# Sums over a head's channels as two fp32r products of split squares, and a pair's values requested after its queries

## The chip, the cores and the metric

The kernel runs on one core of a Trainium2 chip. A core has five engines with their own instruction streams: TensorE (PE in the profile, with its weight loads as PEld), VectorE (DVE), ScalarE (ACT), GpSimd (POOL) and SyncE (SP, which here only issues DMAs). Each works its stream in the order in which it was recorded, and waits on semaphores for the others. The metric is the device time of one execution in microseconds (us). Each kernel's time is a median over several executions.

## The reference

One layer over 528 tokens (16 learned ones and 512 of the input) of 1024 channels, in fp32. A projection of the normed input feeds a recurrent branch (RWKV-7, 8 heads of 64 channels), an attention branch with forgetting (8 heads of 64) and two gates; the branches are mixed and added, and an MLP with squared ReLU follows.

```python
kk = hv(k * k_k)                                   # recurrent branch
kk = kk / jnp.maximum(jnp.sqrt(jnp.sum(kk * kk, axis=-1, keepdims=True)), 1e-12)
...
bonus = jnp.sum(hv(r) * hv(k) * r_k, axis=-1, keepdims=True) * hv(v)

def head_rmsnorm(t, g):                            # queries and keys of attention
    tf = t.astype(jnp.float32)
    return tf * lax.rsqrt(jnp.mean(tf * tf, axis=-1, keepdims=True) + NORM_EPS) * g
```

These are the sums over a head's 64 channels: the length of each recurrent key, the bonus, and the mean square of each query and key.

## The kernel before, in words

Features lie with 128 channels, that is two heads (a "pair"), on the partitions, and tokens along the free dimension. The kernel has three stages. A short first one norms the input and splits it into a high and a low fp32r part (`uhi`, `ulo`). The second, until about 401 us, holds the projections, the recurrence and attention. The third mixes the branches (tiles `po`, `pd`), adds the residual and computes the MLP.

In the second stage products with weights are made as three fp32r products (high by high, high by low, low by high; tile `pj`, line 579), while small products of the branches are single fp32 ones. A sum over a head's channels is a product with `ones_blk`, a 128 by 128 matrix of two blocks of ones, in fp32: line 680 (`pssq`, queries and keys of attention), line 906 (`pkk`, recurrent keys) and line 940 (`pbn`, the bonus, with the matrix scaled by `r_k` beforehand, line 934).

TensorE's order in this stage is recorded by a planner, `Turns`. Each piece of work is a Python generator, a stream: `recurrent` (rank 1), `attention` (2), `fox_features` (3, norms and transposes attention's inputs), `divided` (4, splits the branches' results), `chain` (0), `group_norm` (4) and `projections` (8). A stream yields a function that gives the time when its next input is ready by a cost table; the planner takes the stream of lowest rank that is ready by its own count of TensorE's time. `projections`, ready nearly always, so fills TensorE wherever the others wait. It takes its jobs from a list ordered by rank and request; a job may carry an event (`need`) that must have come before it starts, and then all later jobs stand behind it. The 16 gate blocks (rank 9) are the last of the list. The planner settles TensorE's order; a tile scheduler orders the other engines.

The recurrence treats two groups of two pairs. For each pair it makes `decay`, `keys`, `rows`, `scores` and `bonus`, for a group `inverse`; then the group's `chain` runs over nine chunks, and each chunk is a ring of dependent steps: `pch<-uv,L` (line 1102), a copy on VectorE, `pch<-Rs,Tt` (1108), two copies, `pch<-uv,bkT` (1130), an addition. The chunk's output goes to `py` (1136, 1087). After chunks 4 and 8 `group_norm` works on four chunks: a reduction, a square, a second reduction, eleven tiny steps of an inverse root and a scaling (lines 1146 to 1156), the transposes `pyt` (1161) and products `pg` (1164), then two copies and two operations for each pair (1169 to 1172), whose result is split for the third stage (276). The keys of the fourth pair are requested once the third pair's are normed, and held until that pair's `rows`, which wait for the first chain.

The first products of the third stage are `po` (line 1260); the first of them needs the four recurrent results `ys` that are split last.

Two tiles with one tag share memory in turn. The tags concerned by the change are "KT" (the scaled keys, then a work area of `inverse`), "lc" and "tha" (cumulated decay and gate of the recurrence).

Of the kernel before, what the change touches and what calls it, by code (L numbers as in the profile page):

```python
# [19 lines left out]
T = 528  # L20
NM = 16
S = 512
# [167 lines left out]
def kernel(ctx, tc, ht, x, win, par, cst, gain, lora, wout, wo, wup, wdn, out, dbg=None):  # L190
# [16 lines left out]
    pr = cp.tile([128, N_PAR], F32, name="pr")  # L207
    ident, ones_blk, tmask, cmask = (cs[:, 128 * i:128 * i + 128] for i in range(4))
    mask16 = cs[:, 512:]

# [64 lines left out]
    def split(hi, lo, x):  # L275
        return A.copy(hi, x), V.tensor_tensor(lo, x, hi.bitcast(F32), ALU.subtract)  # L276

    def passes(w, x):
# [9 lines left out]
    with ExitStack() as st:  # L288
# [337 lines left out]
        def forget(prev):  # L626
# [10 lines left out]
            forgot.done = True  # L637

        class Fox:

# [32 lines left out]
            def normed(self, d, parts, gcol):  # L673
                yield d["in"]
                f, sq = d["f"], d["sq"]
                yield lambda: max(ck.ready(sq), banks(len(parts)))
                pin = None
                for a0, a1 in parts:
                    pq = psm("pssq")[:, :a1 - a0]
                    mm(pq, ones_blk, sq[:, a0:a1], start=True, stop=True)  # L680
                    pin = pin or pinned(d["s"])
                    after(act(sq[:, a0:a1], pq, AF.Ln, bias=eps, scale=1.0 / 64), pin)
                c0 = parts[0][0]
# [168 lines left out]
        class Pair:  # L852
# [20 lines left out]
            def decay(self):  # L873
                p = self.p
                lw = load_lora(p, 0, 1)

# [20 lines left out]
            def keys(self):  # L897

                p = self.p
                okr, thr, kp, pinv = self.okk[:, PADT:], self.tha[:, PADT:], self.sg, v9(self.lc)  # L900
                self.sq = sq = rp.tile([128, TP], F32, name="sq")
                s_ = act(sq[:, :T], okr, AF.Square, scale=self.col(C_KK))
                yield lambda: max(ck.ready(sq), banks(2))
                for hc in (slice(0, HT), slice(HT, T)):
                    pq = psm("pkk")[:, :HT]
                    mm(pq, ones_blk, sq[:, hc], start=True, stop=True)
                    V.tensor_scalar(sq[:, hc], pq, 1e-24, None, ALU.max)
# [13 lines left out]
                V.tensor_tensor(KT, BK, self.P[:, :, 63:64].unsqueeze(2).to_broadcast([128, NCH, 2, 64]), ALU.mult)  # L921

            def rows(self):
# [8 lines left out]
                G.tensor_tensor(self.sq[:, :S], self.orr[:, 64:], self.sg[:, 64:], ALU.mult)  # L932
                self.rkb = rp.tile([128, 128], F32, name="rkb")
                after(V.tensor_scalar(self.rkb, ones_blk, self.col(C_RK), None, ALU.mult), last["DVE"])

            def bonus(self):
                rkb = self.rkb
                yield lambda: max(ck.ready(rkb, self.sq), banks(1))
                bp = psm("pbn")
                mm(bp, rkb, self.sq[:, :S], start=True, stop=True)  # L940
                self.bv = bv = rp.tile([128, S], F32, name="bv", bufs=2)
# [3 lines left out]
            def scores(self):  # L945
# [5 lines left out]
                for c0 in range(0, NCH, 3):  # L951
# [14 lines left out]
                    for hs, os in zip(hss, hss[::-1]):  # L966
                        A.copy(bkT[hs, c0:c0 + 3, 64:], pb[os, :3, 64:])

        def inverse(g, Bms, late):


            n2 = 2 * NCH
            Ain = rp.tile([128, 32, 32], F32, name="Ain", tag="Ain")
# [76 lines left out]
            for q in (0, 2):  # L1050
                A.copy(T2[qs[q], :, 32:64], p1[qs[q]])

        def chain(g, prs):
# [555 lines left out]
```

## Time and profile before

| | |
|---|---|
| median of 3 runs | 826.56 us (826.28 to 828.94) |
| the profiled execution | 826.42 us, its span 824.6 us |
| TensorE busy | 808.5 us, 98% |
| VectorE, ScalarE, GpSimd busy | 606.5, 452.7, 120.6 us |
| granted clock of TensorE, mean | 0.998 |
| head sums on TensorE: `pssq`, `pkk`, `pbn` | 8.4, 4.2, 4.1 us |

The page's fifth part groups instructions by source line, engine and tile. [...] An fp32 product shows as two records. The chain of waits follows the work that ended last back through time. In the timeline each row gives start and duration in us, engine, line, operation, output and inputs, shape, count, and in brackets the idle time before it and what ended that.

### The profile page before, as it was taken

How to read it: one execution, taken by the hardware profiler on the slowest of the kernel's cores; microseconds unless marked ns; L12 is line 12 of the kernel's file. 1: busy time of each engine (PE TensorE's matmuls, PEld its weight loads, DVE VectorE, ACT ScalarE, POOL GpSimd, SP SyncE). 2: the span in 40 equal slices, each digit the busy share in tenths (PEclk: the TensorE clock that was granted, in tenths of full speed). 3: DMA queues.
4: the chain of work that ended last, by engine and by line, in shares of the span. 5: the costliest groups of instructions: out<-in, count | busy, mean ns of one | idle time of the engine just before them, and what ended most of it. 6: DMA issues, size and time to landing. Idle time of an engine off the chain costs nothing.

```text
span 824.6 us, 15506 instructions
## 1 busy us (share of the span) xinstructions
PE 808.5 (98%) x5886; PEld 667.4 (81%) x5886; DVE 606.5 (74%) x1196; ACT 452.7 (55%) x941; POOL 120.6 (15%) x124
## 2 busy tenths in 40 slices
PE   8989999998999999999999999999999999999998
PEld 6979887876987787678888889888888888888886
DVE  6787985687879855875366655875698679867988
ACT  7757538756575457754456534664445434543452
POOL 1021100010011000000032003100740074017300
PEclk9999999999999999999999999999999999999999
DMA  7222221211211412223687405523642365337532
GB/s 232 82 71 71 77 92 48 87 40 65 79 52 52 129 41 66 77 78 116 224 287 227 156 0 154 176 80 113 219 149 82 115 208 159 81 115 228 146 99 76
DMA packets 51483, 95.88 MB, mean 116 GB/s; under 512 B 5832, under 2 KB 7240, under 8 KB 51408
## 3 DMA queue, kind: packets, MB, share of 16 engines
q1 hardware_dynamic: 47680, 86.37, 33.2%
q0 software_dynamic: 1280, 4.20, 1.7%
q10 hardware_dynamic: 2448, 4.33, 1.5%
q8 instruction: 46, 0.75, 0.4%
q14 instruction: 29, 0.24, 0.1%
HBM read 88.56 MB, written 6.31 MB: 115 GB/s over the span
## 4 chain that ended last, share of the span: by engine, by line
PE 86%; DVE 5%; ACT 5%; issue 2%; DMA 1%; SPq 0%; POOL 0%; DVEq 0%; ACTq 0%
PE pj L579 22%; PE po L1350 21%; PE po L1477 12%; PE po L1260 5%; PE pd L1477 5%; PE po L1322 3%; PE pj L394 1%; PE po L1291 1%; PE pd L1291 1%; PE psc L748 1%; PE py L802 1%; PE psr L957 1%; PE ppt L785 1%; PE pch L1108 1%; DVE wlo L549 1%
## 5 line engine op out<-in xcount | busy, mean ns | idle before, releaser
L579 PE MATMUL pj<-uhi,whi 128*128 128x264 f32 (+1 forms) x480 | 164.2, 342 | 0.0
L579 PE MATMUL pj<-uhi,wlo 128*128 128x264 f32 (+1 forms) x480 | 153.8, 320 | 2.5 <-DVE wlo L549 2.5
L579 PE MATMUL pj<-ulo,whi 128*128 128x264 f32 (+1 forms) x480 | 153.8, 320 | 0.0
L242 DVE TENSOR_TENSOR wlo<-wraw,whi 128x512 fp32r<-128x512 f32 x84 | 80.3, 966 | 35.5 <-ACT whi L242 35.5
L579 PEld LDWEIGHTS pj<-uhi,whi 128*128 128x128 f32 x480 | 90.7, 189 | 12.8 <-issue 4.4
L579 PEld LDWEIGHTS pj<-uhi,wlo 128*128 128x128 f32 x480 | 90.7, 189 | 9.5 <-DVE wlo L549 2.9
L579 PEld LDWEIGHTS pj<-ulo,whi 128*128 128x128 f32 x480 | 90.9, 189 | 6.7 <-issue 1.6
L1350 PE MATMUL po<-zlo,whi 128*128 128x512 f32 (+1 forms) x248 | 94.8, 382 | 0.0
L1350 PE MATMUL po<-zhi,wlo 128*128 128x512 f32 (+1 forms) x248 | 94.8, 382 | 0.0
L1350 PE MATMUL po<-zhi,whi 128*128 128x512 f32 (+1 forms) x248 | 94.8, 382 | 0.0
L242 ACT CAST whi<-wraw 128x512 fp32r<-128x512 f32 x84 | 51.4, 617 | 55.7 <-PE po L1350 25.6
L548 ACT CAST whi<-wraw 128x512 fp32r<-128x512 f32 x78 | 47.8, 617 | 42.3 <-PE pj L579 41.6
L549 DVE TENSOR_TENSOR wlo<-wraw,whi 128x512 fp32r<-128x512 f32 x78 | 52.7, 685 | 23.7 <-ACT whi L548 23.0
L276 ACT CAST whi<-t 128x512 fp32r<-128x512 f32 x64 | 39.9, 623 | 44.5 <-DVE wlo L276 27.3
L1477 PE MATMUL po<-wlo,fhi 128*128 128x512 f32 (+1 forms) x164 | 63.4, 387 | 0.1
L1399 POOL TENSOR_TENSOR t<-traw 128x512 f32<-128x512 f32 x24 | 38.2, 1608 | 171.6 <-DMA traw<-in_wdn 171.6
L1477 PE MATMUL po<-whi,flo 128*128 128x512 f32 (+1 forms) x164 | 62.9, 384 | 0.0
L1477 PE MATMUL po<-whi,fhi 128*128 128x512 f32 (+1 forms) x164 | 62.3, 384 | 0.0
L276 DVE TENSOR_TENSOR wlo<-t,whi 128x512 fp32r<-128x512 f32 x64 | 43.6, 690 | 24.2 <-ACT whi L276 24.0
L1366 ACT CAST fhi<-R 128x768 fp32r<-128x768 f32 (+1 forms) x32 | 30.2, 944 | 45.2 <-DVE R L1373 25.3
L1350 PEld LDWEIGHTS po<-zhi,wlo 128*128 128x128 f32 x248 | 46.6, 188 | 9.1
L1350 PEld LDWEIGHTS po<-zhi,whi 128*128 128x128 f32 x248 | 46.6, 188 | 9.0
(330 smaller groups left out, 1708.6 us busy)
## 6 DMA issues: line engine op xcount, KB each, us to landing
wraw<-in_win SPq DMA_DIRECT2D x84, 256.0 KB, 2.7
wraw<-in_wup SPq DMA_DIRECT2D x60, 256.0 KB, 3.1
wraw<-in_wdn SPq DMA_DIRECT2D x48, 256.0 KB, 2.7
traw<-in_wdn SPq DMA_DIRECT2D x48, 256.0 KB, 3.5
gd<-gt ACTq DMA_DIRECT2D x16, 256.0 KB, 2.2
wraw<-in_wout SPq DMA_DIRECT2D x16, 256.0 KB, 3.5
gl<-gd SPq DMA_DIRECT2D x16, 256.0 KB, 3.0
traw<-in_wdn POOLq DMA_DIRECT2D x16, 256.0 KB, 3.2
```

The lines of the kernel that those rows point to most:

```text
L242: casts.append((A.copy(hi, raw), low.tensor_tensor(lo, raw, hi.bitcast(F32), ALU.subtract)))
L276: return A.copy(hi, x), V.tensor_tensor(lo, x, hi.bitcast(F32), ALU.subtract)
L548: after(A.copy(hi, raw), last["ACT"])
L549: after(V.tensor_tensor(lo, raw, hi.bitcast(F32), ALU.subtract), last["DVE"])
L579: mm(po, a, b[:, k, a0:a1], start=n == 0, stop=n == 23)
L1260: mm(po, a, ys[k][:, b, :], start=n == 0, stop=n == 11)
L1291: mm(pd[i], a[:, k, 128 * i:128 * i + 128], b, start=k == 0 and n == 0, stop=k == 7 and n == 2)
L1322: mm(po, a[:, k, 128 * i:128 * i + 128], b[:, k, :], start=n == 0, stop=n == 23)
L1350: mm(po[:, t0:t1], a, b[:, k, t0:t1], start=n == 0, stop=n == 23)
L1366: A.copy(fhi[:, j, a:b], R[:, a:b])
L1399: eng.tensor_tensor(t, sums[c, pair] if c in (T1, T2) else c, d, ALU.add)
L1477: mm(x[i][:, cols], a[:, k, left, 128 * rows:128 * rows + 128], c[:, cols], start=start and k == 0 and n == 0, stop=stop and k == n_pairs ...
```

## The change

An fp32r copy `ones_r` of the matrix of ones is made once. Each of the three kinds of sum now splits its squares (for the bonus, the products) into a high part, cast to fp32r on ScalarE, and a low part, the difference, on GpSimd (for the bonus on VectorE), and adds two fp32r products in one accumulation (`summed`). The bonus scales its squares by `r_k` in the split, and the scaled matrix `rkb` is gone. The split parts are kept in memory of other tiles: in "KT" or in "lc" and "tha". Two flags, `held`, see to it that only one stream has each at a time: `decay` takes the second area, `keys`, `bonus` and `inverse` the first, `scores` or `inverse` give it back, and attention's `normed` takes whichever is free, or waits. Apart from that, the values of the second to fourth pair of attention are requested after its queries are normed, and no longer before.

```diff
+    def summed(po, hi, lo):
+        mm(po, ones_r, hi, start=True, stop=False)
+        mm(po, ones_r, lo, start=False, stop=True)
...
+        V.tensor_copy(ones_r, ones_blk)
...
+        held = [0, 0]
+
+        def hold(i):
+            yield lambda: math.inf if held[i] else 0.0
+            held[i] = 1
...
             def normed(self, d, parts, gcol):
                 yield d["in"]
                 f, sq = d["f"], d["sq"]
-                yield lambda: max(ck.ready(sq), banks(len(parts)))
+                c0 = parts[0][0]
+                yield lambda: math.inf if all(held) else 0.0
+                at = held[0]
+                held[at] = 1
+                if at:
+                    hl = rp.tile([128, 2, T], F32R, name="fhl", tag="KT")
+                    hi, lo = hl[:, 0, :], hl[:, 1, :]
+                else:
+                    hi, lo = (rp.tile([128, T], F32R, name="f" + tag, tag=tag) for tag in ("lc", "tha"))
+                d["s"] = A.copy(hi[:, c0:], sq[:, c0:])
+                for a0, a1 in parts:
+                    G.tensor_tensor(lo[:, a0:a1], sq[:, a0:a1], hi[:, a0:a1].bitcast(F32), ALU.subtract)
+                yield lambda: max(ck.ready(lo), banks(len(parts)))
                 pin = None
                 for a0, a1 in parts:
                     pq = psm("pssq")[:, :a1 - a0]
-                    mm(pq, ones_blk, sq[:, a0:a1], start=True, stop=True)
+                    summed(pq, hi[:, a0:a1], lo[:, a0:a1])
...
+                q = yield from x.normed(x.dq, SEQ, qg8)
+                x.q_done.done = True
                 if p > 0:
                     x.ask_values()
-                q = yield from x.normed(x.dq, SEQ, qg8)
-                x.q_done.done = True
...
             def decay(self):
                 p = self.p
+                yield from hold(0)
...
             def keys(self):
 
                 p = self.p
+                yield from hold(1)
...
-                yield lambda: max(ck.ready(sq), banks(2))
-                for hc in (slice(0, HT), slice(HT, T)):
+                hl = rp.tile([128, 2, T], F32R, name="hl", tag="KT")
+                hi, lo = hl[:, 0, :], hl[:, 1, :]
+                s_ = A.copy(hi, sq[:, :T])
+                for hc in parts:
+                    G.tensor_tensor(lo[:, hc], sq[:, hc], hi[:, hc].bitcast(F32), ALU.subtract)
+                yield lambda: max(ck.ready(hl), banks(2))
+                for hc in parts:
                     pq = psm("pkk")[:, :HT]
-                    mm(pq, ones_blk, sq[:, hc], start=True, stop=True)
+                    summed(pq, hi[:, hc], lo[:, hc])
...
             def bonus(self):
-                rkb = self.rkb
-                yield lambda: max(ck.ready(rkb, self.sq), banks(1))
+                yield from hold(1)
+                hl = rp.tile([128, 2, T], F32R, name="hl", tag="KT")
+                hi, lo = hl[:, 0, :S], hl[:, 1, :S]
+                A.activation(hi, self.sq[:, :S], AF.Copy, scale=self.col(C_RK))
+                V.scalar_tensor_tensor(lo, self.sq[:, :S], self.col(C_RK), hi.bitcast(F32), ALU.mult, ALU.subtract)
+                yield lambda: max(ck.ready(hl), banks(1))
                 bp = psm("pbn")
-                mm(bp, rkb, self.sq[:, :S], start=True, stop=True)
+                summed(bp, hi, lo)
+                held[1] = 0
...
         def inverse(g, Bms, late):
 
 
+            yield from hold(1)
```

The flags and the new waits enter the planner's choices, so that TensorE's whole order in the second stage is another one. Two places of it follow. The program's lines are shifted by 6 to 40 in the changed kernel (585 is 579 before, 1300 is 1260).

TensorE at the end of the second stage, before: the last output products of the chain and of attention (`py`), projections (`pj`), the transposes and products of the last group norm (`pyt`, `pg`), projections again, and the first products of the third stage (`po`).

```order
L1087 MATMUL py<-y_fx,Bm 64x64 x4
L799 MATMUL py<-pTm,vm 64x512 x2
...
L802 MATMUL py<-pT_4542,vt 64x128
L579 MATMUL pj<-uhi,whi 128x512
...
L1161 MATMUL pyt<-cs,ysq 128x128 x4
L1164 MATMUL pg<-lhi,lw_4209 128x256
...
L579 MATMUL pj<-uhi,whi 128x512
...
L1260 MATMUL po<-ys,whi 128x512 x2
```

The same end in the changed kernel, from the last projection on:

```order
L585 MATMUL pj<-uhi,wlo 128x512
L1170 MATMUL pch<-uv,bkT 64x64 x4
...
L1142 MATMUL pch<-uv,L_3154 64x64
...
L1148 MATMUL pch<-Rs,Tt 64x64 x4
...
L1142 MATMUL pch<-y_fx,L_3154 64x64
...
L826 MATMUL py<-pT_4918,vt 64x128
L1148 MATMUL pch<-Rs,Tt 64x64 x4
...
L1127 MATMUL py<-y_fx,Bm 64x64 x4
L1201 MATMUL pyt<-cs,ysq 128x128 x4
...
L1204 MATMUL pg<-lhi,lw_4561 128x256
L1300 MATMUL po<-ys,whi 128x512 x2
```

Before, 69 projection products stand ahead of the last group norm's transposes and 57 behind its products; now the last projection stands ahead of the seventh chunk's last step, and two chunks, attention's mixing and two group norms follow with none between.

TensorE at the end of the first chain, before: the eighth chunk's start to the first projection after the chain.

```order
L579 MATMUL pj<-uhi,wlo 128x512
L1102 MATMUL pch<-uv,L_662 64x64
...
L680 MATMUL pssq<-fsq,cs 128x512
L1130 MATMUL pch<-uv,bkT 64x64 x4
...
L748 MATMUL psc<-ka,qa 128x272 x2
L748 MATMUL psc<-ka,qa 128x256 x2
...
L1087 MATMUL py<-y_fx,Bm 64x64 x4
L579 MATMUL pj<-uhi,whi 128x264
```

And now:

```order
L772 MATMUL psc<-ka,qa 128x272 x2
L772 MATMUL psc<-ka,qa 128x256 x2
L1142 MATMUL pch<-uv,L_670 64x64
...
L585 MATMUL pj<-uhi,whi 128x512
...
L1148 MATMUL pch<-Rs,Tt 64x64 x4
L1127 MATMUL py<-uv,Bm 64x64 x4
L1105 MATMUL pvt<-cs,ov 64x128 x2
L585 MATMUL pj<-uhi,whi 128x264
...
L1170 MATMUL pch<-uv,bkT 64x64 x4
```

Before, the 37 rows between the two projections hold none; now projections stand between the chain's steps, up to its last output. Behind the first state product of the second chain lay 240 projection products of 512 columns and 30 of 264 before, and 78 and 48 now.

More of the change, by code (lines that the diff above doesn't have):

```diff
@@ L208 @@
     ident, ones_blk, tmask, cmask = (cs[:, 128 * i:128 * i + 128] for i in range(4))
+    ones_r = cp.tile([128, 128], F32R, name="ones_r")
     mask16 = cs[:, 512:]
@@ L679, in normed @@
                     pq = psm("pssq")[:, :a1 - a0]
-                    mm(pq, ones_blk, sq[:, a0:a1], start=True, stop=True)
+                    summed(pq, hi[:, a0:a1], lo[:, a0:a1])
                     pin = pin or pinned(d["s"])
                     after(act(sq[:, a0:a1], pq, AF.Ln, bias=eps, scale=1.0 / 64), pin)
-                c0 = parts[0][0]
+                held[at] = 0
                 d["s"] = act(sq[:, c0:], sq[:, c0:], AF.Exp, scale=-0.5)
@@ L921, in keys @@
                 V.tensor_tensor(KT, BK, self.P[:, :, 63:64].unsqueeze(2).to_broadcast([128, NCH, 2, 64]), ALU.mult)
+                held[0] = 0
             def rows(self):
@@ L967, in scores @@
                         A.copy(bkT[hs, c0:c0 + 3, 64:], pb[os, :3, 64:])
+                held[1] = 0
         def inverse(g, Bms, late):
+            yield from hold(1)
             n2 = 2 * NCH
@@ L1051, in inverse @@
                 A.copy(T2[qs[q], :, 32:64], p1[qs[q]])
+            held[1] = 0
         def chain(g, prs):
```

3 lines of the change are left out of this document (1 added, 2 removed).

## The prediction

> **What bounds the kernel now.** I read the page first, then the waits of TensorE, then the chain of waits between 350 and 401 us, where the recurrent stage ends.
>
> ```profile
> span 824.6 us, 15506 instructions
> PE 808.5 (98%) x5886; PEld 667.4 (81%) x5886; DVE 606.5 (74%) x1196; ACT 452.7 (55%) x941; POOL 120.6 (15%) x124
> ```
>
> TensorE (PE) is busy for 98% of the span, so its instruction stream, in its recorded order, is the clock of the whole kernel. Two things alone can move the time: PE work, and stretches in which PE's next instruction is not ready. The profiled execution took 826.4 us (span 824.6 and 1.8 around it), 0.1 under the median of the runs, 826.56; my sum starts at 826.4. What keeps PE fed through the recurrent stage are the projection products (pj, L579): they wait for nothing but their weights, and the planner lays them between the links of the slow chains. The chain of waits at the stage's end shows this stock (start, duration, engine, tile, line, count):
>
> ```profile
> 353.55 0.38 PE pch L1130 x8
> ...
> 354.17 1.59 PE pj L579 x6
> ...
> 357.96 2.77 PE pj L579 x12
> ...
> 362.83 1.59 PE pj L579 x6
> ...
> 365.03 0.89 PE pj L579 x3
> ...
> 367.45 0.38 PE py L1087 x8
> 367.83 1.00 PE py L799 x4
> 368.83 2.30 PE py L802 x16
> 371.14 15.89 PE pj L579 x69
> 387.02 0.44 PE pyt L1161 x4
> ...
> 388.18 12.92 PE pj L579 x57
> 401.10 9.07 PE po L1260 x40
> ```
>
> The last state product of the second chain ends at 367.83, attention's last at 371.14; then 69 projections run while VectorE and ScalarE work out the last group norm, and 57 more while its result is scaled and split. At 401.10 the output products (po) start, with all their operands long there. From 353.55 to 401.10 are 47.55 us; projections take 1.59 + 2.77 + 1.59 + 0.89 + 15.89 + 12.92 = 35.65 of them, the other PE rows 11.9.
>
> **The cheaper sums.** TensorE before and after a pair of fp32 sums of 264 columns (first fence), and two fp32 sums of 512 columns (second):
>
> ```profile
> 38.45 1.05 PE L906 MATMUL pkk<-sq,cs 128*128 128x264 f32 x4
> 39.14 0.48 PE L579 MATMUL pj<-uhi,whi 128*128 128x264 f32 x1
> 39.46 0.28 PE L579 MATMUL pj<-ulo,whi 128*128 128x264 f32 x1
> 39.58 0.28 PE L579 MATMUL pj<-uhi,wlo 128*128 128x264 f32 x1
> ```
>
> ```profile
> 65.39 1.02 PE L940 MATMUL pbn<-sq,rkb 128*128 128x512 f32 x2
> 66.25 1.02 PE L680 MATMUL pssq<-fsq,cs 128*128 128x512 f32 x2
> ```
>
> Rows overlap, so I count from start to start. An fp32r product of 264 columns costs 0.12 (39.46 to 39.58), one of 512 columns 15.89/69 = 0.23. The two fp32 sums cost 39.46 - 38.45 = 1.01 less the 0.12 of the projection product in it, 0.89; four fp32r products cost 0.48. There are eight such places (four keys of attention, four of the recurrence): 8 x 0.41 = 3.3 us. A 512-column sum costs 0.86 (65.39 to 66.25) against 2 x 0.23: 0.40 at eight places (four queries, four bonuses), 3.2. The projection after a sum started the next one 0.32 later instead of 0.12, a change of form worth 0.20; it is inside the 264-column price, and at the 512-column places I count 0.5 in all (0 to 1.6). Together **-7.0** (-6.5 to -8.1). All of it lies on PE, hence on the path while there is other PE work to take its place.
>
> **The splits.** Each of the 16 places now needs an extra cast on ScalarE and a subtraction on GpSimd (the bonus: VectorE, in place of scaling a matrix) before PE may sum.
>
> ```profile
> L932 POOL TENSOR_TENSOR sq<-orr,sg 128x512 f32<-128x512 f32 x4 | 7.5, 1876 | 24.4 <-DVE okk L913 15.5 <-DVE rsgy L222 8.6 <-DVE orr L310 0.3
> ```
>
> By this row, 1.88 for 512 columns and half for 264, that is 4 x 1.9 + 16 x 0.95 = 23 us of GpSimd, which the page has busy for 15% of the span; ScalarE, at 55%, has room for 16 casts. GpSimd runs in order: behind a split wait the next block's padding memsets and the BK product that the scores need. With cast and subtraction a place is late by at least the 1.9; uncovered everywhere, 16 x 1.9 = 30 us. The planner lays projections over it: thirty 264-column products (3.6 us) stand between the old and the new place of the first key sum. I charge **+0.9** for what slips through (0, all covered, to 4, a quarter us at each place). The buffers are lent too: while one stream holds "KT", or "lc" and "tha", the others stand. So the second chain comes later in PE's order: 240 projection products of 512 columns and 30 of 264 lay behind its first state product, now 78 and 48: 58.8 us of cover by the prices above has become 23.7.
>
> **The tail without cover.** That difference is spent earlier, and the end is bare: after the last projection come the rest of the seventh chain step, two whole steps, attention's last block, both group norms, and at once the output products. I work out the stretch that took 47.55 us, from the state product at 353.55:
>
> (a) To the end of the last state product (367.83): 14.3 us before, with 6.84 of projections in it. If those only filled time that the links need anyway, 14.3 stays; if they set the pace, 14.3 - 6.84 + 3.3 (attention's mixing, L799 and L802, which now lies inside) = 10.7. I take 12.7: each link's copies queue on VectorE behind attention's softmax, as before.
>
> (b) From there to the group norm's product:
>
> ```profile
> 368.70 0.68 DVE L1146 TENSOR_REDUCE st<-y_rw 128x8 f32<-128x512 f32 x1
> ...
> 374.04 0.69 DVE L549 TENSOR_TENSOR wlo<-wraw,whi 128x512 fp32r<-128x512 f32 x1
> ...
> 377.17 0.69 DVE L1156 TENSOR_TENSOR ysq<-y_rw,rsgy 128x512 f32<-128x512 f32 x1
> ...
> 392.54 0.69 DVE L276 TENSOR_TENSOR ys<-y_rw,ys 128x512 fp32r<-128x512 f32 x1 [0.24 <-ACT ys L276]
> ```
>
> 367.83 to 377.86 is 10.0. The row at 374.04 is the first of two weight splits that stand in between; without them 8.6, without two more splits of that size (other heads' results, as in the last row) 7.2. I take 8.7.
>
> (c) From the group norm's transposes (387.02) to the end of the last split (393.23) are 6.2, 5.5 without the weight split that stood between. Ten of the first twelve output products (10 x 0.23) can run before that split is there: 3.2 to 3.9, I take 3.7.
>
> Sum 25.1 us where PE has 11.9 of its own work: a stall of **+13.2** (9.2 to 16.3).
>
> **The clock.** TensorE's waits, and its clock (last but two) in windows around the longest wait at a chain's end:
>
> ```profile
> PE psc L748 <- DVE nm L759: 1.5, 1, 1.5
> ```
>
> ```profile
> 202.00:204.00 2.00, 1.15 (x4) 0.96 0.00 0
> 204.00:206.00 2.00, 2.00 (x20) 0.50 0.00 0
> 206.00:208.00 2.00, 2.00 (x14) 0.69 0.20 55
> ```
>
> A wait of 1.5 us was followed by a granted clock of 0.50 and 0.69: 2 x (0.04 + 0.50 + 0.31) = 1.7 us of work lost. Step (b) leaves PE idle for over 7 us, so the output products start slow (1.7), and the transposes and products of the group norm, on the path, lose 0.5: **+2.2** (0 if nothing dips; 4.6 with one more dip in the two chain steps, 1.7, and 0.7 on their links). [...]
>
> **The gap that closes.** The wait above came where the first chain ended with no projection among 37 rows of PE. The first block projected after it was a recurrent pair's keys:
>
> ```profile
> 209.88 0.49 DVE L310 SCALAR_TENSOR_TENSOR okk<-pj,pr,tm 128x264 f32<-128x264 f32 x1 [0.80 <-ACT tm L309]
> ```
>
> That job is held until the first chain is done, and stood first in line. Now the second group's keys are normed later against the chain, the held job comes to the front later, and projections lie in that place. So the wait and its dip go: **-3.2** (0 to -3.2). The values asked for later are three jobs that go past gate jobs, each with two weight loads on SyncE, two casts and two splits, covered by the same stock; if one came late, attention's transposes would (within the 4 above).
>
> Sum: 826.4 - 7.0 + 0.9 + 13.2 + 2.2 - 3.2 = **832.5 us**.
>
> **The rivals.** A difference under 0.3% (2.5 us) can't be told from none here. *Forecast: bare tail, slower*, chance 0.62, own range 829.2 to 836.5. *Faster*: with VectorE and ScalarE freed of weight splits, the last two steps and the norm close up, and the savings stand. It decides once the stall is under 7 us: with 6.0 and no dip, 826.4 - 7.0 - 3.2 + 6.0 + 0.9 = 823.1. For it: those engines have less to do in the tail. Against: my low end, 9.2, has foreign work taken out already. 0.10. *No change*: the stall is at that low end, 9.7 with the waits, and no dip: 826.4 - 10.2 + 9.7 + 0.4 = 826.3. For it: at 354 to 366 us projections followed every link, so links may be faster than they look. 0.18. *Slower still*: the lent buffers stall streams in mid-stage, the old gap gets a successor (0 gained), the tail is 14.5 with 3.2 of dips and 1.5 of waits: 826.4 - 7.0 + 14.5 + 3.2 + 1.5 = 838.6. For it: 16 new places wait for GpSimd, whose rows vary. 0.10.
>
> Faster 0.10, same 0.18, slower 0.62 + 0.10 = 0.72. The bounds alone give 824 to 845; the range leaves out the faster case and most of the last: 826.0 to 838.5.
>
> **What would show it.** Cheaper sums: PE busy down by about 7 us, pssq, pkk and pbn at 0.12 or 0.23 per product. Bare tail: no pj row in the last 25 us before the first po row, ten or more us of PE waits there on VectorE and ScalarE rows of the chain and the group norm, and a granted clock near 0.5 as po begins. Closed gap: no PE wait on nm near 200 us. I am wrong if PE's idle time between the last pj and the first dense po rows is under 8 us, or if PE shows new waits on hl, flc or ftha of several us.

## The result, and the profile after

The changed kernel takes 833.79 us (median of 4 runs, 833.13 to 835.41), the kernel before 827.34 (4 runs, 826.28 to 828.94): a ratio of 1.0071, with a 95% interval from 1.0049 to 1.0092. It is slower by 0.7%. The profiled execution took 833.66 us against 826.42, its span 831.9 against 824.6, so 7.3 us are to be found in it.

The head of the changed kernel's page:

```profile
span 831.9 us, 15539 instructions
PE 804.7 (97%) x5886; PEld 667.5 (80%) x5886; DVE 609.1 (73%) x1197; ACT 460.9 (55%) x957; POOL 136.2 (16%) x144
```

TensorE is busy for 3.8 us less, and its span is longer. The first output product of the dense row starts at 401.10 before and at 407.54 now; what follows takes 423.5 and 424.4 us. So the second stage holds nearly all of it. TensorE up to that product and behind it, before and then after (columns: window, its width, busy time, records, granted clock, DMA share, GB/s):

```profile
0.00:401.10 401.10, 388.93 (x3947) 1.00 0.27 83
401.10:824.60 423.50, 419.57 (x1941) 1.00 0.47 147
```

```profile
0.00:407.54 407.54, 384.33 (x3947) 0.98 0.26 84
407.54:831.90 424.36, 420.35 (x1940) 1.00 0.46 145
```

Width less busy time is idle time: 12.2 us before, 23.2 now. A second loss hides in busy time, the clock: in windows of 2 us, busy time times what the clock lacks of 1.00 sums to 1.7 before and 4.5 now. What is left I call work: 387.3 and 379.9. So the stage became 7.4 us lighter in work, and it lost 11.0 in waits and 2.8 in clock.

TensorE's waits now (line, what ended the wait; us in total, times, longest):

```profile
PE pyt L1201 <- DVE ysq L1196: 8.9, 1, 8.9
PE pw L1068 <- issue: 3.3, 2, 1.9
...
PE py L1176 <- ACT y_rw L1128: 1.2, 2, 0.8
PE psr L994 <- DVE tm L311: 1.1, 1, 1.1
```

The first row is the wait for the last group norm, which 15.89 us of projections covered before. The second is new in kind: TensorE stopped twice inside a burst of small products (lines 1065 and 1068, the inverse of each pair group), and the profile shows nothing that it waited for. The old first rows, wlo and nm, are gone from the list. No row names a split part (hl, fhl, flc, ftha).

The end of the stage in windows, from the last projection on (columns as above):

```profile
382.63:398.00 15.37, 11.35 (x145) 1.00 0.11 36
398.00:400.00 2.00, 0.00 (x0) 0.75 0.00 0
400.00:405.17 5.17, 0.00 (x1) 0.50 0.00 0
405.17:407.54 2.37, 2.37 (x11) 0.50 0.00 0
407.54:411.00 3.46, 3.46 (x12) 0.75 0.00 0
```

TensorE is idle for 4.0 + 2.0 + 5.2 = 11.2 us there, and the norm's products and the first output products then run at half clock.

### The profile page after: what moved, and what is told of

It reads as the page before. It is cut to its first block, busy times and chain, and to the rows that moved or that the text cites. A ratio compares the mean times of both kernels' runs of the same rounds, so it can differ in the third digit from the quotient of the medians.

```text
span 831.9 us, 15539 instructions
## 1 busy us (share of the span) xinstructions
PE 804.7 (97%) x5886; PEld 667.5 (80%) x5886; DVE 609.1 (73%) x1197; ACT 460.9 (55%) x957; POOL 136.2 (16%) x144
## 4 chain that ended last, share of the span: by engine, by line
PE 86%; DVE 7%; ACT 4%; issue 2%; DMA 1%; SPq 1%; DVEq 0%; ACTq 0%
PE pj L585 23%; PE po L1390 21%; PE po L1517 12%; PE po L1300 5%; PE pd L1517 5%; PE po L1362 3%; PE pj L399 1%; PE pd L1331 1%; PE po L1331 1%; PE py L826 1%; PE psc L772 1%; PE psr L994 1%; PE ppt L809 1%; PE pch L1148 1%; DVE wlo L555 1%
## 5 line engine op out<-in xcount | busy, mean ns | idle before, releaser
L585 PE MATMUL pj<-uhi,whi 128*128 128x264 f32 (+1 forms) x480 | 162.3, 338 | 0.8 <-DVE orr L315 0.8
L555 DVE TENSOR_TENSOR wlo<-wraw,whi 128x512 fp32r<-128x512 f32 x78 | 52.9, 690 | 23.2 <-ACT whi L554 22.8
L1390 PEld LDWEIGHTS po<-zlo,whi 128*128 128x128 f32 x248 | 46.6, 188 | 9.0
```

The source lines that it names most:

```text
L555: after(V.tensor_tensor(lo, raw, hi.bitcast(F32), ALU.subtract), last["DVE"])
L585: mm(po, a, b[:, k, a0:a1], start=n == 0, stop=n == 23)
L1390: mm(po[:, t0:t1], a, b[:, k, t0:t1], start=n == 0, stop=n == 23)
```

## The experiments

Each was timed against the kernel before on the same chip. The account of the stage, made as above, for all of them (us; the last column is the rest after idle time and clock, good to a few us only: e5 and e6 have 3946 records of the same products in the same order in it and come to 381.1 and 385.2). A trace is one execution, and the granted clock differs among the executions of one kernel: of 51 executions of the kernel before that were timed beside the experiments, the 13 with a mean clock of 0.998 took 826.7 us on average, the 24 with 0.996 took 828.6. The traced one has 0.998. So a difference of 2 us in the clock column can come from the execution that was traced, and not from the kernel.

| kernel | median | ratio to before | first output product | idle | clock | work |
|---|---|---|---|---|---|---|
| before | 827.34 | 1 | 401.1 | 12.2 | 1.7 | 387.3 |
| changed | 833.79 | 1.0071 | 407.5 | 23.2 | 4.5 | 379.9 |
| e1 values alone | 834.25 | 1.0072 | 408.6 | 14.5 | 6.4 | 387.6 |
| e2 sums alone | 834.27 | 1.0076 | 409.2 | 19.8 | 10.4 | 379.0 |
| e3 reserve | 839.70 | 1.0138 | 411.9 | 23.5 | 10.5 | 378.0 |
| e4 rounded, new plan | 828.84 | 1.0007 | 403.9 | 13.0 | 6.8 | 384.1 |
| e5 rounded, old order | 821.58 | 0.9917 | 395.8 | 11.3 | 3.4 | 381.1 |
| e6 split, old order | 846.22 | 1.0211 | 421.2 | 23.1 | 12.9 | 385.2 |
| e7 same, on VectorE | 843.48 | 1.0181 | 418.1 | 23.3 | 9.6 | 385.2 |
| e8 tail filled (7.7 of the work is filling) | 832.54 | 1.0057 | 407.6 | 15.3 | 4.0 | 388.2 |
| e9 fp32, new order | 834.04 | 1.0071 | 407.9 | 19.4 | 2.8 | 385.7 |
| e10 tail covered | 831.94 | 1.0045 | 408.4 | 19.9 | 8.4 | 380.1 |
| e11 one product, old order | 818.71 | 0.9884 | 393.8 | 13.8 | 3.3 | 376.7 |
| e12 shifted | 832.79 | 1.0050 | 403.2 | 19.9 | 2.8 | 380.6 |

### The two parts, each alone

e1 moves only the request of the values; e2 makes only the sums, with their splits and flags.

```diff
-                if p > 0:
-                    x.ask_values()
                 q = yield from x.normed(x.dq, SEQ, qg8)
                 x.q_done.done = True
+                if p > 0:
+                    x.ask_values()
```

> The kernel before with the second part of the change alone: values asked for after the queries are normed, sums as before. Theory A (the time follows TensorE's work and how much of the chain's end has projections behind it): its order still has 16.7 us of projections between the second chain's end and the last group norm's transposes and 9.7 us behind them, and the work is the same, so 825.5 to 829, no difference to tell. Rival B (the asking order itself starves attention and stalls TensorE): 830 or more.

> The changed kernel with values asked for before the queries are normed, as formerly; splits, lent buffers and the cheaper sums all stay. Theory A: work is 7.5 us less than before, and the order has 12.4 us of projections at the last group norm and none after it, so of the 25 us tail only some 3 us are bare: 821 to 825, faster than before. Rival B (splits and lending stall the streams, wherever the projections stand): near the changed kernel, 831 to 835.

Measured: 834.25 us, 1.0072 (1.0048 to 1.0096), and 834.27, 1.0076 (1.0054 to 1.0097). Theory A missed both times, and the times lie in the rivals' ranges: each part alone is as slow as the two together. The parts do not add up, so it can't be the tail's cover alone; and of e2's waits only one of 0.2 us names a split part. In e1 TensorE has the work of before, and waits and clock that before did not have. Its waits, and its clock around them:

```profile
PE pyt L1161 <- DVE ysq L1156: 2.9, 1, 2.9
PE pj L579 <- DVE wlo L549: 2.5, 1, 2.5
PE ppm L783 <- ACT pm L768: 2.3, 1, 2.3
```

```profile
52.00:56.00 4.00, 4.00 (x34) 0.57 0.74 231
182.00:185.00 3.00, 0.33 (x3) 1.00 0.00 0
185.00:189.00 4.00, 4.00 (x33) 0.57 0.01 4
```

Each of the three waits is followed by half clock. Windows laid on these stretches show 0.50 for 3.41 us behind the first two in time and for 6.83 behind the third, so they cost 1.7 to 3.4 us beside their own length. That is not fixed: the wait for wlo stands in the kernel before at the same place and with the same length (2.47 us there, 2.46 here), and the 2 us behind it ran at 1.00:

```profile
52.00:54.00 2.00, 2.00 (x19) 1.00 0.58 170
```

In e2 the tail has no wait at all; the largest one stands at 117 us, where the inverse's VectorE work comes late for TensorE:

```profile
PE pw L1059 <- DVE AX L1045: 6.9, 1, 6.9
PE pw L1068 <- issue: 2.1, 2, 1.2
```

What the three kernels share is only that the planner made a new order for the stage. That became the new theory A: the order, not the parts, costs the time.

### A reserve for the tail

In the changed kernel three gate blocks may start only when the second chain is done.

```diff
-            ask(9, B_GATE + i, gate_job(i), SEQ)
+            ask(9, B_GATE + i, gate_job(i), SEQ, need=chained[1] if i > 12 else None)
```

> The changed kernel with its last three gate blocks (16.6 us of projections) held back until the second chain has ended. Theory A (cover misplaced): the 11.6 us of stall and 3.7 us of slow clock at the last group norm go, but six chunks of the chain now have no projections between their steps, at about 1 us of stall each: 824 to 829. Rival (the stage has become bound by the length of the chain of splits and steps, not by where projections stand): what is gained at the end is lost in the chunks, 831 to 835.

Measured: 839.70 us, 1.0138 (1.0117 to 1.0159), slower than the changed kernel and than both answers. 72 projections now stand behind the chain (first fence, the chain of waits), and the chunks before it are bare (second fence, TensorE's waits):

```profile
394.19 16.55 PE pj L585 x72
```

```profile
PE ppt L807 <- ACT pm L792: 3.3, 1, 3.3
PE ppm L807 <- ACT pm L792: 2.6, 1, 2.6
```

The clock lost 10.5 us. The reserve was planned at the cost of the links. So cover matters in the links too, and a planner that decides anew can't test one place by itself; the later experiments replay an order.

### Sums without splits, planner free

The values are asked for as in the changed kernel, the squares are rounded to fp32r where they are made, and both products take them, with a matrix of halves; the low parts are left out.

```diff
+    def summed(po, x, w=None):
+        w = ones_r if w is None else w
+        mm(po, w, x, start=True, stop=False)
+        mm(po, w, x, start=False, stop=True)
```

> The kernel before with values asked later and each sum as two fp32r products, but of the rounded squares twice, times one half: no split, no lent buffer, no wait between streams. Left out are the low parts of the squares, and what is made in their place (logarithm, root) is rounded too; the bonus's factor is applied on VectorE in the product. Theory A: TensorE's work as in the changed kernel, 7.5 us under before, and 24 us of projections at the last group norm: 818 to 822. If the sums on TensorE were not worth 7.5 us: 825 to 829. If fp32r products in place of fp32 ones cost something else (form changes, weights): above 829.

Measured: 828.84 us, 1.0007 (0.9993 to 1.0022), the answer by which the sums are not worth 7.5 us. No wait at the last norm, no wait for a split, and still none of the saving: it fell to the clock (6.8 us against 1.7) and, by the account, to work.

### The order of before, replayed

For e5, e6, e7 and e11 I recorded which stream the planner took at each of its 562 choices in the kernel before, and the bank of each projection, and replayed them. The order of TensorE is then that of before, row for row, but for the sums.

```diff
-            at = next((i for i, t in enumerate(times) if t + self.ROOM[self.streams[i][0]] <= ck.pe + ck.SLACK), None)
+            at = [x[1] for x in self.streams].index(int(ORDER[self.step], 16))
+            self.step += 1
```

> The planner's choices of the kernel before are replayed one by one, so that every engine keeps the order of the kernel before; only the three kinds of sum are two fp32r products each. The low parts are left out: squares are rounded to fp32r where they are made, and both products of a sum take the same rounded operand with a matrix of halves, so no split has to be waited for. Values are asked for as before. Theory A (order): the cheaper sums save their 7.0 to 7.5 us of TensorE work in any order, and what ate the saving in all four earlier kernels are the waits and the half-clock stretches that a new order of the second stage brings; in the old order those stay what they were (12.2 and 1.7 us), so 818 to 822. Theory B (links): the recurrence's links set the pace, and what a sum saves comes back as a wait at the next link in any order: 824 to 828.

Measured: 821.58 us, 0.9917 (0.9903 to 0.9932), 6.9 us under before (0.0083 of 828): theory A. The waits stay those of before:

```profile
PE pj L595 <- DVE wlo L564: 1.9, 1, 1.9
PE pbt L977 <- DVE KT L937: 1.9, 2, 1.1
PE pch L1121 <- DVE Rs L1117: 1.8, 3, 1.2
```

The sums are those of e4, at the same cost; the order, with the place at which values are asked for, makes 7.3 us between the two kernels. (The values' request alone was not tried in the old order: there the transposes of a pair's values stand ahead of the place to which their projection would move.) e11 goes on in that order, with one product per sum:

> Order of the kernel before and rounded squares as in the kernel that ran in 821.6 us, but with one fp32r product per sum in place of two; the low parts are left out here too. It takes away 16 products of 264 columns at 0.12 and 8 of 512 at 0.23, 3.8 us of TensorE work. Order theory: 821.6 - 3.8 = 817.8 (816 to 819.5). Links theory: most of it comes back as waits at the next links: 820.5 to 823.

Measured: 818.71 us, 0.9884 (0.9872 to 0.9897): 2.9 us less than e5 where 3.8 us of work were taken out. It lies in theory A's range; three quarters of the work became time. e5 and e11 beat both kernels, with sums of rounded squares; no kernel with the full sums was faster than before.

e6 has the full sums in the old order (cast on ScalarE, difference on GpSimd, in memory that is free at each place), e7 the differences on VectorE:

```diff
-                    G.tensor_tensor(lo[:, a0 - c0:a1 - c0], sq[:, a0:a1], hi[:, a0 - c0:a1 - c0].bitcast(F32), ALU.subtract)
+                    V.tensor_tensor(lo[:, a0 - c0:a1 - c0], sq[:, a0:a1], hi[:, a0 - c0:a1 - c0].bitcast(F32), ALU.subtract)
```

> Order of the kernel before as in the last kernel, with full sums: high and low parts as in the changed kernel (cast on ScalarE, difference on GpSimd), in memory that is free at each place, so no flag holds a stream. The sums stand where they stood, with no further projections laid ahead of them, so at seven of the sixteen places TensorE has to wait for cast and difference. From the end of the square to the start of the sum in the kernel before (0.2 to 1.3 us of slack) and 1.7 to 2.7 us for cast and first difference, these waits are 2.4, 1.6, 2.4, 1.2, 1.4, 1.2, 2.4, together 12.6 us. Theory A: 819.4 + 12.6 = 832, less where later waits shrink by it, more by a half-clock stretch of 1.7 after each wait over 1.5: 828 to 836, and TensorE's waits name hl and fhl. Theory B: the sums' places are links of the same chain, so 828 to 836 too, but with the old waits gone from the list; if the splits are covered (as the prediction charged them, 0.9), 819 to 823.

> As the last kernel, with the differences on VectorE instead of GpSimd and the casts made half by half, so that the first product of a sum is late by about 0.8 us instead of 1.7 to 2.7 (a VectorE difference of 512 columns takes 0.69 in the row of wlo, 264 columns about 0.4). Waits left by the same slacks: 0.6, 0.3, 0.9, 0, 0.2, 0, 1.0, together 3 us. Theory A: 819.4 + 3 = 820 to 825, the first kernel with the full computation that is faster than before. Theory B: 825 to 831, since saved work comes back as waits and the splits add to VectorE, which the chain steps need.

Measured: 846.22 us, 1.0211 (1.0192 to 1.0230), and 843.48, 1.0181 (1.0166 to 1.0197). Both ranges missed, on the slow side. e6's waits:

```profile
PE pssq L289 <- POOL fhl L700: 4.2, 4, 1.3
PE pkk L289 <- POOL hl L934: 3.8, 5, 1.6
PE pssq L288 <- ACT fhl L698: 3.7, 2, 2.3
PE pbn L289 <- DVE hl L970: 2.2, 2, 1.2
PE pch L1141 <- DVE Rs L1137: 1.8, 3, 1.3
PE pbn L288 <- ACT hl L969: 1.7, 2, 0.9
```

The split parts are waited for 15.6 us (4.2 + 3.8 + 3.7 + 2.2 + 1.7) instead of 12.6, partly at places where I had found slack: TensorE waits 5.4 us (3.7 + 1.7) for casts, which stand in ScalarE's queue behind other work. What I had charged with one dip or none was the clock: 12.9 us, 9.5 more than e5. Against e5 the first output product is 25.4 us later, for 11.8 us more of idle time. Moving the difference to VectorE shortens some waits and lengthens others (pssq to 8.6 in all), since VectorE, busy for 606.5 us in the kernel before, has other work in front. So at the places of the old sums the splits cost more than the sums save. In the changed kernel the planner lays projections over them, and no wait names them.

### The changed kernel's order, with the old sums

> The planner's choices of the changed kernel are replayed one by one, with its flags, but the three kinds of sum are single fp32 products as before, and no splits are made. With the earlier kernels this completes a table of two orders by two kinds of sum. Order theory: order and sums add up, so the changed kernel's 833.8 plus the 7.0 to 7.5 us of TensorE work that come back: 839 to 843 (up to 1 less if a wait for a split goes). Links theory: in the changed kernel's order TensorE waits anyway, so dearer sums fill waits: 833 to 836.

Measured: 834.04 us, 1.0071 (1.0051 to 1.0091). The order theory missed here: in the new order the dearer sums cost nothing. With e5 the table is complete:

| | fp32 sums | fp32r sums |
|---|---|---|
| order of before | 827.34 | 821.58 (rounded) |
| order of the change | 834.04 | 833.79 (split) |

So cheaper sums are worth 6.9 us in one order and 0.3 in the other, and the new order by itself costs what the change costs. The two entries of the right column are not the same sums: split ones take 846.22 in the old order (e6), and rounded ones in the new order were not run, so how much of the 0.3 is owed to the splits is not shown. By the account, the dearer sums bring 5.8 us of work to the new order and take 3.8 of idle time and 1.7 of clock away. Where, shows when the same instructions of the two kernels are set side by side. At the inverse's second burst (132.1 us) e9 runs 1.08 us behind the changed kernel, as dearer sums should make it; at 142.6 it is 1.73 ahead. In between the changed kernel stops in the burst, and e9 does not. First the changed kernel's row, then e9's:

```profile
136.32 0.85 PE L1068 MATMUL pw<-Tt,AX 32*32 32x32 f32 x42 [1.33 <-issue]
```

```profile
135.13 1.49 PE L1063 MATMUL pw<-Tt,AX 32*32 32x32 f32 x128
```

Behind the break the changed kernel's clock falls, and so it does behind its second break, of 1.95 us, which ends at 315.88:

```profile
136.00:138.00 2.00, 1.68 (x46) 0.55 0.04 8
138.00:140.00 2.00, 2.00 (x7) 0.60 0.00 0
...
316.00:318.00 2.00, 2.00 (x20) 0.77 0.04 8
318.00:320.00 2.00, 2.00 (x6) 0.50 0.00 0
320.00:322.00 2.00, 2.00 (x67) 0.87 0.40 123
```

The two breaks and their clock cost the changed kernel 1.33 + 1.95 + 2 x 1.7 = 6.7 us. e9 has the second one too, at 1.1 us; so 2.2 us of breaks and about 1.7 of clock are what the dearer sums spare, and the rest of the 5.5 is shorter waits.

### What stops TensorE in the bursts

The page lists a DMA queue of its own kind, and a window of 0.5 us shortly ahead of the second break, 313.0 to 313.5, shows one of its packets (packets, MB, share of 16 engines):

```profile
q8 instruction: 46, 0.75, 0.4%
```

```profile
q8 instruction: 1, 0.02, 14.4%
```

46 packets of 0.75 MB in all are 16 KB each, and TensorE's 5886 products and as many weight loads are 256 to a packet. In narrower windows this packet starts at 313.2, and the break ends at 315.88, 2.7 us later; the one at 133.7 is followed by the break's end at 136.32, 2.6 later. The same holds in all eight kernels with such breaks: fifteen of them end 2.3 to 2.9 us after a packet starts, and the next packet starts 1.0 to 1.6 after the break's end (1.1 both times in the changed kernel). Counted in the traces, with the waits for semaphores (17 and 49 ahead of the changed kernel's two breaks), each of the fifteen comes after 2497, 5825, 6081 or 6337 of TensorE's instructions (2497 and 6337 there), numbers that lie whole multiples of 256 apart: every break stands on a boundary between blocks. The boundaries before these two are, by the same count, at 132.70 and 312.23. So from the first instruction of one block until the next block was there it took 3.62 and 3.65 us. In these bursts 192 records, 384 instructions, run in 3.3 us when nothing stops them (e12, 134.33 to 137.60). e12 leaves the order and shifts TensorE's blocks against its bursts:

```diff
-                for i in range(8):
+                for i in range(6):
                     mm(warm[:, :128], ones, ones, start=True, stop=True)
+                for i in range(32):
+                    mm(warm[:32, :32], ones[:32, :32], ones[:32, :32], start=True, stop=True)
...
-            for n, pr_, c in cells:
+            for n, pr_, c in (cells[:7] if g == 0 else []) + cells:
```

> The changed kernel with its order replayed, and TensorE's instructions shifted in their stream: 32 products of 32 by 32 at the start in place of two of the eight warm-up products (120 instructions more), and 14 of the 32 products of the last burst of the first pair group's inverse recorded twice (57 more), their second results the same as the first. The traces of the earlier kernels show TensorE's 11,772 instructions coming in 46 packets of 16 KB, 256 in each, and every break without a releaser in the bursts of 32 by 32 products ends 2.3 to 2.9 us after such a packet starts, in eight kernels. Fetch theory: a stretch of 256 instructions that runs in less than about 3.7 us waits for its successor; in the changed kernel the boundaries fall 69 and 57 per cent into such a stretch in the bursts, behind the shift they fall into the projections beside them. Both breaks (3.3 us) and their half-clock stretches (3.4) go, 0.5 us of products come: 826 to 829.5, and no row with issue as releaser at the bursts. Rival (the bursts themselves, or weight loads beside them, stall TensorE): the breaks stay, 833 to 835.

Both breaks are gone from its trace, with their clock:

```profile
136.31 1.29 PE L1082 MATMUL pw<-Tt,AX 32*32 32x32 f32 x128
...
312.40 1.29 PE L1082 MATMUL pw<-Tt,AX 32*32 32x32 f32 x128
```

The packets now start at 137.5 and 313.4, and the blocks they bring are needed only in the projections that follow. The profiled execution took 829.44 us, 4.2 less than the changed kernel's and inside the expected range; a half-clock stretch of 3.41 us at 56 us, which the changed kernel's trace does not have, takes back 1.7 of what the breaks and their clock gave. The median is 832.79, 1.0050 (1.0033 to 1.0067), outside the range, and the other five executions took 830.88 to 834.57. So the cause of the breaks is shown in the trace, but a gain of the whole is not: the intervals of e12 and of the changed kernel overlap, and what the executions without a trace lost stays open. Their mean clock does not tell it: 0.992 went with 829.44 and with 834.57.

### The tail

e8 lays 34 products that nobody reads ahead of the last group norm's transposes; e10 replays the changed kernel's order with nine steps of projections taken out between 358 and 383 us, seven put ahead of those transposes and two behind the norm's products.

```diff
+            if g == 1 and c0 == 4:
+                fill = ps.tile([128, 512], F32, name="fill", tag="ch", bufs=1)
+                for i in range(34):
+                    mm(fill, ones_r, uhi[:, 0, :512], start=True, stop=True)
```

> The changed kernel with 34 products of 512 columns that nobody reads (7.7 us of the 8.9 us in which TensorE waited for the last group norm) ahead of the last group norm's transposes, so that TensorE stays busy there and the granted clock does not fall. Clock theory (the prediction's term of 2.2): without them the transposes, the group norm's products and the first output products ran at 0.50 and lost 2.5 us; with the clock at 1.00 the time is 830 to 832. Rival: the splits of the last results set the start of the output products and the clock costs nothing there: 833 to 834.5. If the fill itself is late, above 835.

Measured: 832.54 us, 1.0057 (1.0039 to 1.0076), between the two answers. e8's tail (start, duration, row):

```profile
406.42 0.63 PE L1205 MATMUL pyt<-cs,ysq 128*128 128x128 f32 x4 [0.81 <-DVE ysq L1196]
407.61 0.62 PE L1304 MATMUL po<-ys,whi 128*128 128x512 f32 x2
410.40 0.73 PE L1304 MATMUL po<-ys,whi 128*128 128x512 f32 x2 [0.36 <-ACT ys L277]
...
410.60 1.46 DVE L277 TENSOR_TENSOR ys<-y_rw,ys 128x512 fp32r<-128x512 f32 x2
```

At full clock (1.00 from 405 to 411 us) ten output products run at once, and TensorE then waits 0.36 us for a cast; part of what half clock costs is time in which it would have waited for the last splits. The median gained 1.25; in the traces the stretch from the norm's transposes to the end is 426.7 us in the changed kernel and 425.3 here.

The end of the list of choices that e10 replays, before and with the edit (each character is a stream, 5 the projections):

```
a992292929924444bb14
9a992292929924444b5555555b5514
```

> The changed kernel with its order replayed, except that nine steps of projections (27 products of 512 columns, 6.1 us) are taken out of places between 358 and 383 us where two or more such steps stand in a row, seven of them put ahead of the last group norm's transposes and two behind its products. Nothing else is moved. Bare-tail theory: the projections taken away only filled time behind which the links still have one step each, so the chain ends up to 6 us earlier, the wait of 8.9 us falls to about 4, the clock dips for less: 826 to 829. Rival: the steps taken out covered links that need the time (the prediction's upper bound for the end of the chain), so gaps open at their old places and the time stays at 832 to 834.

Measured: 831.94 us, 1.0045 (1.0025 to 1.0064), at the rival's edge; the trace says why. In its execution the half-clock stretches behind both breaks were twice as long (6.83 us for 3.41; the breaks themselves took 3.1 us together, for 3.3), so that it entered the tail's part 3.1 us behind the changed kernel (at 357.6 us of that one); from there it gained 4.55 us and reached the last group norm 1.45 ahead. So 6.1 us of projections taken out of the links brought 4.55: they mostly filled time. The wait for the norm fell less than by their 4.8 us:

```profile
PE pyt L1213 <- DVE ysq L1208: 5.5, 2, 4.3
```

and of it 4.3 at the last norm. VectorE's rows there, with the norm's first reduction and its subtraction as first and last:

```profile
395.16 0.68 DVE L1198 TENSOR_REDUCE st<-y_rw 128x8 f32<-128x512 f32 x1
395.87 0.69 DVE L288 TENSOR_TENSOR ys<-py,ys 128x512 fp32r<-128x512 f32 x1
...
397.75 0.69 DVE L254 TENSOR_TENSOR wlo<-wraw,whi 128x512 fp32r<-128x512 f32 x1
398.36 0.68 DVE L1200 TENSOR_TENSOR y_rw<-y_rw,st 128x512 f32<-128x512 f32 x1
```

Three splits of other results and one of weights stand in between, 2.5 us. The mechanism is the forecast's; its gain did not come out whole, since this execution lost more clock behind the breaks. The intervals of e8 and of e10 overlap the changed kernel's, so neither gain is shown by the medians; what is said of the tail rests on the traces.

## Why the prediction was right, and where not

The forecast, a bare tail, 832.5 us, came within 1.2 us of the profiled execution. Its sign holds, and the longest wait stands where it put it, at a bare tail. Its terms, against the account:

- **Cheaper sums, -7.0.** TensorE's work fell by 7.4, within its bounds. The products cost what was read from the rows:

```profile
41.84 0.28 PE L280 MATMUL pkk<-hl,ones_r 128*128 128x264 f32 x1
41.96 0.28 PE L281 MATMUL pkk<-hl,ones_r 128*128 128x264 f32 x1
```

  The sentence that all of it lies on the path failed, though: it is time in the old order (6.9 of it, e5), and next to nothing in the new one (e9), where TensorE stops in the bursts and waits longer elsewhere. By the sum of the prediction, e9, without the cheaper sums and their splits, would have taken 832.5 + 7.0 - 0.9 = 838.6; it took 834.04.
- **The splits, +0.9.** Right as covered: no wait names them. What can be seen of them is indirect: TensorE waits 0.96 us for `BK` at 53.35, which e9 does not, and the VectorE operation that makes it starts 0.6 us earlier there. e6 gives the price without the cover, 25 us where the prediction had bounded it by 30 and charged no clock. The cover is what the tail then lacked.
- **The bare tail, +13.2.** 11.2 measured, inside 9.2 to 16.3. Step (a) took 13.6 (12.7 taken), from 382.63 to 396.23, and step (b) 8.9 (8.7), from there to 405.17. Step (c) is the mis-sized one: in e8 410.40 - 406.42 = 4.0, less ten products of 0.23, are 1.7, where 3.7 stood. The last split ends 5.6 us after the transposes start, as assumed (5.5 to 6.2), but TensorE has more than ten products to run before it needs it. Together 24.2 for 25.1; the rest of the 2.0 is 0.7 more of TensorE's own work than 11.9, and the 0.36 of waiting that half clock hid.
- **The clock, +2.2.** In the tail 2.37 x 0.50 + 3.46 x 0.25 = 2.05. Not all of it is on the path: by the traces e8 gave back 1.4. The dips elsewhere in the stage came after the breaks and were not in the sum.
- **The gap that closes, -3.2.** This is the step that failed. The wait on nm and its dip at 200 us, shown in the prediction, are gone as it said. But the two breaks took its place, with 3.3 us and 3.4 of clock, of which the prediction knew nothing; with some shorter waits gone, the middle of the stage lost 7.3 + 7.4 - 11.2 - 2.05 = 1.4 where the sum had 0.9 - 3.2 = -2.3. That 3.7 too little, and 2.0 + 0.15 too much for the tail and its clock, and 0.4 too little for the sums' saving, make the 1.2: the total owes part of its closeness to errors that cancel.

The rival of links that close up (823.1) is out by the 11.2 us of the tail. The rival of no change (826.3) had a stall of 9.7 and no dip; stall and dips in the tail were 11.2 and 2.05, and the middle of the stage gave nothing back. The rival of lent buffers that stall streams (838.6) had its place right in part, the middle of the stage, but what was lost there were breaks in bursts, and no wait names a lent buffer. What no rival had is that either part alone would cost as much (e1, e2).

How long a wait must be to cost the clock, the runs do not show. The breaks of 1.33 and 1.95 us above, and e1's wait of 2.3, were each followed by a stretch at 0.50. So was a break of only 0.55 us in e4, while 2.47 us in the kernel before was not:

```profile
279.66 0.85 PE L1033 MATMUL pw<-Tt,AX 32*32 32x32 f32 x76 [0.55 <-issue]
```

The clock behind it was 0.50 from 280.62 to 284.03. So in these kernels the length of the wait alone does not tell whether it costs the clock.

## What to carry to other kernels

Where a planner writes the order, a small edit changes all of it, and the edit's own saving drowns in that: with the same cheap sums, two orders lay 7.3 us apart here (e4 and e5), as much as the sums could save. To know what an edit is worth, replay the old order with it, and the new order without it; only then change the planner. And price a wait of TensorE with the clock that may follow it: here half clock took 1.7 us and more, after a wait of 0.55 us as after one of 8.9, and nothing after others.

## What the runs showed of the hardware

In the second stage of the kernel before and of the changed one the granted clock is 1.00 or 0.50. The stretches at 0.50 are 3.41 us long in the kernel before (203.82 to 207.24) and behind both breaks of the changed one (136.18 to 139.59 and 317.09 to 320.50). Behind a wait of e1 and behind the breaks of e10 they are 6.83, twice that, and at the changed kernel's tail 10.24 (399.01 to 409.25), three times that. In the changed kernel's second one, projections of 512 columns start 0.43 us apart (317.64 to 318.07) where they start 0.23 apart ahead of it (316.47 to 316.70), so 3.41 us that TensorE works through cost 1.7. The same waits can bring such a stretch or not: those for `BK` and `KT` near 55 us, 0.97 and 0.78 us, did in e12 and, at 0.96 and 0.78, did not in the changed kernel.

In these traces TensorE's instructions arrive in 46 blocks of 16 KB, 256 instructions each, over a queue that the page lists. In the changed kernel it took 3.62 and 3.65 us from the start of one block until the next could run, so the two dense bursts of tiny products (64 in 1.29 us in e12's rows, 20 ns each) outran their own code. Whether they did depended on where the block's boundary fell: in e12, 120 and 176 instructions more ahead of the two bursts removed both breaks.
